# A running logsumexp along time: three steps per partition, Exp written over its input, and one stream of chunks

## The chip, the core and the metric

One core of one Trainium2 chip. The time is device microseconds of one launch; medians of several runs are given. The profile's span is about 1.8 us shorter than the time of the run.

The engines' names: PE is the matrix engine, ACT the one that computes Exp and Ln, DVE the vector engine, SP the one whose queue issues all DMA transfers here. "The DMA records of the trace" are the starts, durations and sizes of the single packets that the 16 DMA engines moved. What I say of single packets is read from these. They don't name the engine.

## The reference

```python
# x: (4, 4096, 4128) float32, standard normal
out[:, 0, :] = x[:, 0, :]
for t in range(1, S):
    mx = np.maximum(out[:, t - 1, :], x[:, t, :])
    out[:, t, :] = mx + np.log(np.exp(out[:, t - 1, :] - mx) + np.exp(x[:, t, :] - mx))
```

That is a running sum of exp(x) along time, and its logarithm. 270.5 MB are read and 270.5 MB written.

## The kernel before

A tile holds R = 2 consecutive time steps on each of 128 partitions, so a partition's part of a transfer is one run of 2 x 4128 x 4 = 33,024 B. ACT writes Exp in fp16 to its own buffers; PE adds along the partitions with triangular matrices of ones (`incl`, `excl`), adds the running sum of the tiles before (`pick` times `carry`) and, for the second step, the second row (`ident`); ACT takes Ln from PSUM into the tile; DVE saves the last row's sum in two fp16 parts (`keep`).

```python
R = 2
xpool = ctx.enter_context(tc.tile_pool(name="xpool", bufs=5))
epool = ctx.enter_context(tc.tile_pool(name="epool", bufs=4))
# ... (cut)
class Step:
    def __init__(self, b, k):
        self.xt = xpool.tile([P, R, D], FP32, name="xt")
        self.dram = lambda t: t[b, k * rows:(k + 1) * rows, :].rearrange("(p j) d -> p j d", j=R)
        nc.sync.dma_start(out=self.xt, in_=self.dram(x))          # load
    def exp(self, c):
        et = epool.tile([P, R, CH + tail], FP16, name="et")
        nc.scalar.activation(et[:, :, :w], self.xt[:, :, s], ACT.Exp)
    # ... (cut: head, second, tail)
    def ln(self, j, c):
        nc.scalar.activation(self.xt[:, j, c * CH:(c + 1) * CH], self.pt[c], ACT.Ln)
    def store(self):
        nc.sync.dma_start(out=self.dram(out), in_=self.xt)
    def run(self):                       # one tile from its first Exp to its store
        self.exp(0); self.head(0)
        for c in range(1, n_main):
            ...                          # (cut)
        self.store()

for i, (b, k) in enumerate(work):        # 64 tiles
    if i == 0:
        steps += [Step(*work[n]) for n in range(3)]
    if i + 3 < len(work):
        steps.append(Step(*work[i + 3])) # the load of tile i+3 stands before the store of tile i
    steps[i].run()
```

The softmax here doesn't subtract the row's maximum and nothing guards it: scores larger than these inputs give would overflow.

## Time and profile before

| | before |
|---|---|
| time, median | 1265.67 us (three runs, 1265.14 to 1265.82) |
| bytes moved by DMA | 541 MB |
| ACT, PE, DVE busy | 962.5, 663.4, 655.7 us of 1263.8 |
| data packets | 16,384 of 33,024 B, median 1222 ns |

From the profile's page of the kernel before: span, busy times, moved GB/s in 40 slices, the data queue (packets with the completions, MB, share of the engines' time), the chain that ended last, the Exp instructions (count, busy us, mean ns; then idle time before them and its cause), and the transfers with their median time from issue to landing.

```profile
span 1263.8 us, 7025 instructions
...
PE 663.4 (52%) x2392; PEld 242.3 (19%) x2392; DVE 655.7 (52%) x645; ACT 962.5 (76%) x833; POOL 2.2 (0%) x13
...
GB/s 401 418 433 429 434 431 430 433 431 432 430 435 434 430 434 432 434 431 431 432 434 434 432 433 433 432 431 434 434 429 434 435 433 429 433 435 431 431 435 322
...
q1 hardware_dynamic: 18432, 541.07, 99.4%
...
DMA 81%; ACT 2%; issue 1%; PE 1%; DVE 1%; SPq 1%; ACTq 0%
...
L111 ACT ACTIVATE et<-xt 128x2048 f16<-128x2048 f32 (+1 forms) x256 | 485.4, 1921 | 152.8 <-DMA xt<-in_x_dram 152.8
...
xt<-in_x_dram SPq DMA_DIRECT2D x64, 4128.0 KB, 29.4
out_dram<-xt SPq DMA_DIRECT2D x64, 4128.0 KB, 38.8
```

Nearly every slice moves 429 to 435 GB/s; only the first two (401 and 418) and the last (322) fall behind. No compute engine is busy for more than 76% of the span, and ACT's largest idle time before Exp is a wait for loads. The chain is 81% DMA. Each load lands 29.4 us after its issue though a transfer of this size takes 4128 x 1024 B / 432 GB/s = 9.8 us: about two others lie before it in the queue.

A stretch of 200 us in the middle (its length; busy us and count of each engine; granted PE clock; DMA busy share; GB/s):

```profile
core 0: us, PE busy (x) PEld busy (x) DVE busy (x) ACT busy (x) POOL busy (x), PEclk, DMA share, GB/s
900.00:1100.00 200.00, 104.72 (x379) 38.41 (x380) 104.33 (x103) 152.72 (x133) 0.00 (x0) 0.77 1.00 432
```

DMA is busy all of the time at 432 GB/s. The same view of the end of the run:

```profile
1230.00:1240.00 10.00, 5.62 (x24) 2.03 (x23) 4.91 (x4) 7.90 (x8) 0.00 (x0) 0.83 0.99 429
1240.00:1245.00 5.00, 0.51 (x2) 0.02 (x1) 4.05 (x5) 1.82 (x3) 0.00 (x0) 0.72 1.01 438
1245.00:1250.00 5.00, 0.00 (x0) 0.00 (x0) 1.25 (x2) 0.00 (x0) 0.00 (x0) 0.50 0.98 423
1250.00:1255.00 5.00, 0.00 (x0) 0.00 (x0) 0.00 (x0) 0.00 (x0) 0.00 (x0) 0.50 0.87 376
1255.00:1260.00 5.00, 0.00 (x0) 0.00 (x0) 0.00 (x0) 0.00 (x0) 0.00 (x0) 0.50 0.28 119
```

The rate falls step by step after 1250 us: the 16 DMA engines do not finish together. In the DMA records they finish between 1250.9 and 1260.7 us after the first packet, the slowest 9.8 us behind the first.

### The profile page before, as it was taken

To read this page: it belongs to the slowest core of one execution; us is meant where nothing else is said; L and a number is where in the kernel's file an instruction comes from. 1 tells how busy PE (TensorE), PEld (TensorE's weight loads), DVE (VectorE), ACT (ScalarE), POOL (GpSimd) and SP (SyncE) were. 2 spreads that over 40 slices of the span, in tenths; PEclk is the share of its full clock that TensorE was granted. 3 is DMA by queue.
4 is the path that set the end of the run, shared out by engine and by line. 5 is a ranking of instruction groups with operands and counts; after the bars stand their busy time and mean duration, and the time that the engine had idled before them with its cause. 6 is when DMAs were issued, how large, how long until landed. Compare 5 with 4: busy or idle time off the path is not lost.

```text
span 1263.8 us, 7025 instructions
## 1 busy us (share of the span) xinstructions
PE 663.4 (52%) x2392; PEld 242.3 (19%) x2392; DVE 655.7 (52%) x645; ACT 962.5 (76%) x833; POOL 2.2 (0%) x13
## 2 busy tenths in 40 slices
PE   3665655545545465464454655556445464554541
PEld 1222222211112121121121211112112121121210
DVE  3566565464454544645546455464564544545443
ACT  5889887778678787786877877778778787787872
POOL 0000000000000000000000000000000000000000
PEclk8878788778687777777867777777777777777876
DMA  9999999999999999999999999999999999999997
GB/s 401 418 433 429 434 431 430 433 431 432 430 435 434 430 434 432 434 431 431 432 434 434 432 433 433 432 431 434 434 429 434 435 433 429 433 435 431 431 435 322
DMA packets 18466, 541.51 MB, mean 428 GB/s; under 512 B 2048, under 2 KB 2048, under 8 KB 2048
## 3 DMA queue, kind: packets, MB, share of 16 engines
q1 hardware_dynamic: 18432, 541.07, 99.4%
q8 instruction: 19, 0.31, 0.1%
q14 instruction: 15, 0.12, 0.0%
HBM read 270.53 MB, written 270.53 MB: 428 GB/s over the span
## 4 chain that ended last, share of the span: by engine, by line
DMA 81%; ACT 2%; issue 1%; PE 1%; DVE 1%; SPq 1%; ACTq 0%
DMA out_dram<-xt 74%; DMA xt<-in_x_dram 7%; ACT xt L126 1%; ACT et L111 1%; PE pt L86 1%; SPq L102 1%; DVE carry L90 0%; DVE carry L91 0%; SPq L153 0%; DVE carry_t L90 0%; DVE carry_t L91 0%; ACTq L126 0%
## 5 line engine op out<-in xcount | busy, mean ns | idle before, releaser
L90 DVE CAST carry<-pt 32x1024 f16<-32x1024 f32 x256 | 314.9, 1230 | 576.4 <-ACT xt L126 573.3
L111 ACT ACTIVATE et<-xt 128x2048 f16<-128x2048 f32 (+1 forms) x256 | 485.4, 1921 | 152.8 <-DMA xt<-in_x_dram 152.8
L126 ACT ACTIVATE xt<-pt 128x1024 f32<-128x1024 f32 x512 | 504.2, 1028 | 125.8 <-PE pt L86 64.9
L86 PE MATMUL pt<-et,incl 128*128 128x512 f16 x512 | 211.6, 506 | 549.4 <-ACT et L111 386.0
L91 DVE TENSOR_TENSOR carry<-pt,carry 32x1024 f16<-32x1024 f32 x256 | 314.0, 1226 | 8.9
L86 PE MATMUL pt<-et,excl 128*128 128x512 f16 x512 | 211.3, 505 | 0.0
L86 PEld LDWEIGHTS <-incl 128*128 128x128 f16 x704 | 69.0, 111 | 684.7 <-issue 631.9
L86 PE MATMUL pt<-carry,pick 128*128 128x512 f16 x480 | 195.2, 498 | 0.0
L86 PE MATMUL pt<-et,ident 128*128 128x512 f16 x512 | 174.4, 426 | 27.7 <-ACT xt L126 27.7
L86 PEld LDWEIGHTS <-excl 128*128 128x128 f16 x576 | 71.2, 124 | 116.1 <-issue 83.9
L86 PEld LDWEIGHTS <-pick 128*128 128x128 f16 x600 | 69.5, 118 | 94.4 <-issue 66.0
L86 PEld LDWEIGHTS <-ident 128*128 128x128 f16 x512 | 49.5, 106 | 102.4 <-issue 76.4
L86 PE MATMUL qt<-et,incl 128*128 128x32 f16 x192 | 19.6, 189 | 0.0
L86 PE MATMUL qt<-carry_t,pick 128*128 128x32 f16 x120 | 15.6, 182 | 0.0
L149 ACT ACTIVATE xt<-qt 128x64 f32<-128x64 f32 x64 | 14.6, 228 | 0.0
L90 DVE CAST carry_t<-qt 32x32 f16<-32x32 f32 x64 | 12.6, 197 | 2.0
L91 DVE TENSOR_TENSOR carry_t<-qt,carry_t 32x32 f16<-32x32 f32 x64 | 12.4, 193 | 2.2
L86 PE MATMUL qt<-et,excl 128*128 128x32 f16 x64 | 11.6, 182 | 0.0
L81 DVE MEMSET carry<- 128x512 uint32 x4 | 1.9, 485 | 1.1 <-PEq L199 1.0
L68 ACT ACT_TABLE_LOAD x1 | 1.3, 1283 | 0.8 <-PEq L199 0.8
L35 POOL TENSOR_SCALAR_AFFINE_SELECT pick<-pick 128x128 f16<-128x128 f16 x2 | 0.6, 292 | 0.1
L25 POOL TENSOR_SCALAR_AFFINE_SELECT incl<-incl 128x128 f16<-128x128 f16 x1 | 0.3, 293 | 0.0
(11 smaller groups left out, 1.9 us busy)
## 6 DMA issues: line engine op xcount, KB each, us to landing
xt<-in_x_dram SPq DMA_DIRECT2D x64, 4128.0 KB, 29.4
out_dram<-xt SPq DMA_DIRECT2D x64, 4128.0 KB, 38.8
```

The lines of the kernel that those rows point to most:

```text
L25: nc.gpsimd.affine_select(out=t, in_=t, pattern=[[1, P]], compare_op=mybir.AluOpType.is_ge, fill=0.0, base=base, channel_multiplier=-1,)
L35: nc.gpsimd.affine_select(out=t, in_=t, pattern=[[step, P]], compare_op=mybir.AluOpType.not_equal, fill=1.0, base=base, channel_multiplier=1,)
L68: nc.scalar.preload_act_table_set("natural_log_exp_and_others")
L81: nc.vector.memset(t, 0.0)
L86: nc.tensor.matmul(pt, lhsT=w, rhs=rhs, start=start, stop=stop, skip_group_check=True)
L90: nc.vector.tensor_copy(cr[HI:HI + 32, :], pt[HI:HI + 32])
L91: nc.vector.tensor_tensor(out=cr[LO:LO + 32, :], in0=pt[HI:HI + 32], in1=cr[HI:HI + 32, :], op=mybir.AluOpType.subtract,)
L102: nc.sync.dma_start(out=self.xt, in_=self.dram(x))
L111: nc.scalar.activation(et[:, :, :w], self.xt[:, :, s], ACT.Exp)
L126: nc.scalar.activation(self.xt[:, j, c * CH:(c + 1) * CH], self.pt[c], ACT.Ln)
L149: nc.scalar.activation(self.xt[:, :, t0:D], self.qt, ACT.Ln)
```

## The change

The intent was longer runs, so fewer packets and transfers. Three time steps per partition make runs of 49,536 B. To fit four such tiles in SBUF, Exp writes its fp16 result over the first half of the chunk's own float32 bytes, and the Exp buffers go. The chunks of all tiles form one stream, in which Exp runs two chunks ahead, across tile borders. 32 groups of 128 rows are not divisible by three: each batch has ten tiles of three rows and one of two, 44 tiles instead of 64. The diff, cut to its core:

```diff
-R = 2
+R = 3
-    xpool = ctx.enter_context(tc.tile_pool(name="xpool", bufs=5))
-    epool = ctx.enter_context(tc.tile_pool(name="epool", bufs=4))
+    bufs = 4
+    xpool = ctx.enter_context(tc.tile_pool(name="xpool", bufs=bufs))
@@ Exp over its input
-            et = epool.tile([P, R, CH + tail], FP16, name="et")
-            nc.scalar.activation(et[:, :, :w], self.xt[:, :, s], ACT.Exp)
+            nc.scalar.activation(
+                self.t.half[:, :, 2 * c0:2 * c0 + w], self.t.xt[:, :, c0:c0 + w], ACT.Exp,
+            )
@@ one stream of chunks   (cut: head, stage, the tile list)
-        steps[i].run()
+    ahead = bufs - 1
+    for s in steps[:ahead]:
+        s.load()
+    chunks[0].exp()
+    chunks[1].exp()
+    chunks[0].head()
+    for g in range(len(chunks) + R - 1):
+        for d in range(R - 1, -1, -1):
+            if 0 <= g - d < len(chunks) and d < chunks[g - d].t.r:
+                k = chunks[g - d]
+                k.stage(d)
+                if k.c == last and d + 1 == k.t.r:
+                    k.t.store()
+                    if stored + ahead < len(steps):
+                        steps[stored + ahead].load()
+                    stored += 1
+        if g + 2 < len(chunks):
+            chunks[g + 2].exp()
+        if g + 1 < len(chunks):
+            chunks[g + 1].head()
```

The load of tile i+3 now stands behind the store of tile i.

## The prediction

> What bounds the kernel now: the 16 DMA engines. The page's slices show DMA at 9 in all but the last slice and 430 to 435 GB/s almost throughout, except the first (401) and last (322). The table of stretches gives a DMA share of 1.00 and 432 or 433 GB/s in each 200 us stretch from 100 to 1100 us. The chain that ended last is 81% DMA. The compute engines have slack: ACT 76% (962.5 us), PE 52%, DVE 52%; ACT idles 152.8 us waiting for loads (groups list). In the trace's DMA records each of the 16,384 data packets (one 33,024 B run) has a median of 1222 ns: 27.02 B/ns, or 432.4 GB/s on 16 engines. So each engine works 1024 x 1.222 = 1251.3 us on data, plus 128 completion packets of 9 ns (1.2 us). The other 11 us of the 1263.8 us span are the start, collisions with instruction fetches, and a ragged end in which the engines finish at different times (376, 119, then 17 GB/s after 1250 us).
>
> What the change does:
> - Bytes: unchanged, 541 MB. No gain there.
> - Packets: 704 per engine instead of 1024, of 49,536 B (33,024 B in the short tiles). The Trainium skill, "DMA: Bandwidth & Descriptors", "Where 436 GB/s comes from", gives 16 ports x 32 B x 850 MHz. From it I estimate 1214 ns for 33,024 B, so the measured 1222 ns leaves about 8 ns fixed per packet. Then a 49,536 B packet takes about 1829 ns: 640 x 1.829 + 64 x 1.222 = 1249 us, a saving of 2.3 us; 40 fewer completions save 0.4 us.
> - Alignment: 49,536 is 193.5 x 256, so every second run starts 128 B off a 256 B boundary (before, none did). The same page, "How a descriptor splits into AXI transactions", makes that 4 extra beats; I estimate 5 ns on half of the packets, 1.5 us given back.
> - ACT: Exp is one instruction of 3 x 1024 instead of 2 x 1024 (1901 ns now; estimate 2.8 us), 512 Ln of 1028 ns stay. DVE keeps the carry 44 times instead of 64 per chunk: 655 us falls to about 450. PE: about the same total. All this is off the critical path: worth nothing.
> - Buffers: four of 49.5 KB, three loads ahead. A load waits for the previous tile's store, and a store waits for Exp of the next tile's first two chunks. By my count the queue still holds about two transfers (14.6 us each) whenever the next is issued, and a store is ready some 10 us after the next tile's load, with 29 us to spare. At the start three loads cover 41 us and the first store comes at about 36. No new bubble.
>
> On the critical path lies only the per-packet cost: net 1 to 3 us of 1265.
>
> Predicted: 1263.5 us, 8 in 10 between 1257 and 1270. Faster by over 2%: 0.02; within 2%: 0.95; slower by over 2%: 0.03.
>
> What would show it: q1 data packets 11,264 instead of 16,384; packet median near 1830 ns; stretches still 432 to 434 GB/s at share 1.00; DVE near 450 us; ACT still waiting for loads; load landing about 44 us, store about 58 us instead of 29.4 and 38.8.
>
> What would make it wrong: larger packets running at another rate (unaligned HBM writes dearer than a few beats, or another fixed cost per packet); a bubble in the DMA queue, slices below 425 GB/s, because the load waits in order behind a store that waits for the next tile's Exp; engines finishing more unevenly.

## More of the kernel before

I followed each engine through packets that begin where another ends, so numbers of one engine are a reconstruction. "Mean idle time" is the time without a packet under way, averaged over the 16 engines; it needs no such following.

Last, what SP's queue waited for (us in total, times, longest):

```profile
SPq L102 <- DMA out_dram<-xt: 1079.6, 59, 19.2
SPq L153 <- ACT xt L126: 90.5, 8, 18.2
```

SP waits for a buffer, that is, for an earlier store to land, and only rarely for ACT. Stores are ready well before the queue gets to them.

## The result, and the profile after

The changed kernel took 1262.84 us (median of 4 runs, 1262.66 to 1263.26) against 1265.69 us for the kernel before in the same rounds. The ratio is 0.9979, 95% interval 0.9961 to 0.9996: 2.8 us less, the same within 2%. A repetition on another occasion gave 1263.02 against 1265.59 us, again 0.9979.

The same parts of the page, for the changed kernel:

```profile
span 1261.0 us, 6165 instructions
...
PE 688.7 (55%) x2268; PEld 237.0 (19%) x2268; DVE 451.4 (36%) x445; ACT 947.3 (75%) x733; POOL 2.2 (0%) x13
...
GB/s 411 410 439 431 432 427 434 438 430 432 433 437 431 432 432 436 432 427 436 431 433 436 437 429 431 436 436 432 430 434 435 432 431 432 434 435 431 433 422 347
DMA packets 12702, 541.46 MB, mean 429 GB/s; under 512 B 1408, under 2 KB 1408, under 8 KB 1408
...
q1 hardware_dynamic: 12672, 541.07, 99.4%
...
DMA 69%; ACT 21%; PE 5%; issue 2%; DVE 1%; SPq 0%; ACTq 0%
...
L128 ACT ACTIVATE xt<-xt 128x3072 f16<-128x3072 f32 (+3 forms) x176 | 478.5, 2719 | 247.9 <-DMA xt<-in_x_dram 247.8
...
xt<-in_x_dram SPq DMA_DIRECT2D x40, 6192.0 KB, 42.2
out_dram<-xt SPq DMA_DIRECT2D x40, 6192.0 KB, 28.1
```

The slices still show 427 to 439 GB/s nearly throughout; the first two and the last two are lower. Of the 12,672 packets of the data queue 1408 are completions, 16 for each of the 88 transfers, and 11,264 carry data. DVE fell from 655.7 to 451.4 us and ACT from 962.5 to 947.3 us, and neither mattered. A load lands 42.2 us after its issue, three transfers of 14.6 us. A store lands 28.1 us after its issue, two transfers of that size, where the kernel before had four smaller ones.

The middle (columns as before):

```profile
900.00:1100.00 200.00, 109.86 (x361) 38.01 (x361) 72.18 (x72) 151.67 (x118) 0.00 (x0) 0.77 1.00 433
```

The same busy share and the same rate. The end:

```profile
1230.00:1240.00 10.00, 6.73 (x22) 2.31 (x22) 7.75 (x8) 9.29 (x9) 0.00 (x0) 0.83 0.63 269
1240.00:1245.00 5.00, 1.90 (x12) 0.72 (x10) 4.84 (x6) 3.13 (x4) 0.00 (x0) 0.93 1.08 466
1245.00:1250.00 5.00, 0.00 (x0) 0.00 (x0) 1.64 (x2) 0.00 (x0) 0.00 (x0) 0.50 0.98 423
1250.00:1255.00 5.00, 0.00 (x0) 0.00 (x0) 0.00 (x0) 0.00 (x0) 0.00 (x0) 0.50 0.98 423
1255.00:1260.00 5.00, 0.00 (x0) 0.00 (x0) 0.00 (x0) 0.00 (x0) 0.00 (x0) 0.50 0.73 317
```

Here is something that was not there before. The rate falls to 269 GB/s between 1230 and 1240 us, recovers, and then stops at once, without the long thinning out. What SP waited for:

```profile
SPq L116 <- ACT xt L162: 1178.4, 44, 30.0
SPq L113 <- DMA out_dram<-xt: 14.3, 4, 4.9
```

SP waits for ACT, almost all of the time, and hardly ever for a buffer: the stores have become late. The chain near the end of the run (start us, duration, what) says why:

```profile
1124.26 42.48 DMA xt<-in_x_dram
...
1166.77 2.76 ACT xt L128
...
1183.04 37.65 DMA xt<-in_x_dram
```

A load is issued at 1124.26 us and lands at 1166.75. ACT's time line after it (start us, us, instruction; in brackets the idle time before it; L128 is Exp, L162 is Ln):

```profile
1166.77 2.76 ACT L128 ACTIVATE xt<-xt 128x3072 f16<-128x3072 f32 x1 [6.10 <-DMA xt<-in_x_dram]
...
1173.52 2.75 ACT L128 ACTIVATE xt<-xt 128x3072 f16<-128x3072 f32 x1
...
1178.88 2.79 ACT L128 ACTIVATE xt<-xt 128x3072 f16<-128x3072 f32 x1
1181.54 2.87 ACT L162 ACTIVATE xt<-pt 128x1024 f32<-128x1024 f32 x3
```

Three Exp of the new tile run, with Ln of the older one between them. Only after the first of the last three Ln shown comes the store of the older tile, at 1182.61 us, with the next load behind it, as SP's own time line says:

```profile
37.00 0.35 SPq L116 DMA_DIRECT2D out_dram<-xt  x1
...
1153.25 0.34 SPq L116 DMA_DIRECT2D out_dram<-xt  x1
1153.68 0.38 SPq L113 DMA_DIRECT2D xt<-in_x_dram  x1
1182.61 0.34 SPq L116 DMA_DIRECT2D out_dram<-xt  x1
1183.04 0.38 SPq L113 DMA_DIRECT2D xt<-in_x_dram  x1
```

A store is issued 1182.61 - 1166.75 = 15.9 us after the next tile's load has landed. The order of the code agrees: before the last Ln of a tile stand three Exp of the next one, not two.

From the DMA records, the median duration of a packet by its size, in all kernels:

```
bytes    ns     seen in
 8,256   312    one-engine experiment (runs start on 256 B boundaries)
16,512   615    the two padded kernels
33,024  1222    before, and the short tiles after
49,536  1829    after
```

From 33,024 to 49,536 B it is 607 ns more, 27.20 B/ns, which on 16 engines is 435.2 GB/s. That is just the ceiling in the Trainium skill, "DMA: Bandwidth & Descriptors", "Where 436 GB/s comes from". On this line 33,024 B alone take 1214 ns, so about 8 ns of each packet don't depend on its size.

### The profile page after: what moved, and what is told of

Its sections match the earlier page's. It is cut to its first block, busy times and chain, and to the rows that moved or that the text cites. A ratio compares the mean times of both kernels' runs of the same rounds, so it can differ in the third digit from the quotient of the medians.

```text
span 1261.0 us, 6165 instructions
## 1 busy us (share of the span) xinstructions
PE 688.7 (55%) x2268; PEld 237.0 (19%) x2268; DVE 451.4 (36%) x445; ACT 947.3 (75%) x733; POOL 2.2 (0%) x13
## 2 busy tenths in 40 slices
DMA packets 12702, 541.46 MB, mean 429 GB/s; under 512 B 1408, under 2 KB 1408, under 8 KB 1408
## 3 DMA queue, kind: packets, MB, share of 16 engines
q1 hardware_dynamic: 12672, 541.07, 99.4%
## 4 chain that ended last, share of the span: by engine, by line
DMA 69%; ACT 21%; PE 5%; issue 2%; DVE 1%; SPq 0%; ACTq 0%
DMA xt<-in_x_dram 67%; ACT xt L128 11%; ACT xt L162 10%; PE pt L88 5%; DMA out_dram<-xt 2%; ACT xt L167 0%; SPq L116 0%; DVE carry L92 0%; DVE carry L93 0%; ACTq L231 0%; SPq L113 0%; ACTq L128 0%; PE qt L88 0%
## 5 line engine op out<-in xcount | busy, mean ns | idle before, releaser
L128 ACT ACTIVATE xt<-xt 128x3072 f16<-128x3072 f32 (+3 forms) x176 | 478.5, 2719 | 247.9 <-DMA xt<-in_x_dram 247.8
L88 PE MATMUL pt<-xt,ident 128*128 128x512 f16 x672 | 251.3, 470 | 530.7 <-ACT xt L162 530.4
L162 ACT ACTIVATE xt<-pt 128x1024 f32<-128x1024 f32 x512 | 487.6, 1030 | 2.5 <-PE pt L88 0.7
L92 DVE CAST carry<-pt 32x1024 f16<-32x1024 f32 x176 | 216.4, 1230 | 761.0 <-ACT xt L162 760.7
L88 PE MATMUL pt<-xt,excl 128*128 128x512 f16 x672 | 247.0, 504 | 0.0
L93 DVE TENSOR_TENSOR carry<-pt,carry 32x1024 f16<-32x1024 f32 x176 | 215.9, 1227 | 6.1
L88 PE MATMUL pt<-xt,incl 128*128 128x512 f16 x352 | 152.0, 526 | 23.6 <-ACT xt L128 15.0
L88 PEld LDWEIGHTS <-excl 128*128 128x128 f16 x756 | 92.5, 124 | 141.0 <-issue 108.1
L88 PE MATMUL pt<-carry,pick 128*128 128x512 f16 x320 | 109.8, 429 | 0.0
L88 PEld LDWEIGHTS <-incl 128*128 128x128 f16 x480 | 45.2, 111 | 129.7 <-DVE carry L93 95.2
L88 PEld LDWEIGHTS <-pick 128*128 128x128 f16 x360 | 40.6, 113 | 57.0 <-issue 34.3
## 6 DMA issues: line engine op xcount, KB each, us to landing
xt<-in_x_dram SPq DMA_DIRECT2D x40, 6192.0 KB, 42.2
out_dram<-xt SPq DMA_DIRECT2D x40, 6192.0 KB, 28.1
```

What stands on the lines that cost most here:

```text
L88: nc.tensor.matmul(pt, lhsT=w, rhs=rhs, start=start, stop=stop, skip_group_check=True)
L92: nc.vector.tensor_copy(cr[HI:HI + 32, :], pt[HI:HI + 32])
L93: nc.vector.tensor_tensor(out=cr[LO:LO + 32, :], in0=pt[HI:HI + 32], in1=cr[HI:HI + 32, :], op=mybir.AluOpType.subtract,)
L128: nc.scalar.activation(self.t.half[:, :, 2 * c0:2 * c0 + w], self.t.xt[:, :, c0:c0 + w], ACT.Exp,)
L162: nc.scalar.activation(t.xt[:, j, c * CH:(c + 1) * CH], pt, ACT.Ln)
```

## The experiments

Theory: the DMA engines' own work (packets and transfers) gained the time, and the slowest DMA engine sets the end. Rivals: the new order of compute or the in-place Exp gained it; or mean DMA idle time near the end counts, so that the new hole costs something. Times below are medians, with the kernel before in the same rounds at 1265.4 to 1265.6 us.

### Copies without compute, two and three rows

```diff
-    chunks = [Chunk(s, c) for s in steps for c in range(n_main)]
-    # ... the stream
+    for i, s in enumerate(steps):
+        s.store()
+        if i + ahead < len(steps):
+            steps[i + ahead].load()
```

Their outputs are wrong, which doesn't matter for the times. The first has R = 2, the second R = 3, both four buffers.

> Only the loads and stores of the changed kernel with two rows per partition (33,024 B packets); no compute, so the result is wrong on purpose. Packet theory (the change saved about 8 ns on each of 320 packets and 9 ns on each of 40 completions per engine): packets 1222 ns, 1024 per engine, and the time is 2.9 us (2.5 to 3.3) above the copy with three rows. Rival (the saving came from the new order of work or its instructions, not from the packets): the two copies agree within 1 us. Absolute time about 1259 us if instruction fetches are what makes engines finish unevenly, 1263 or more if they are not.

> The same copy with three rows per partition (49,536 B packets). Packet theory: 1829 ns a packet, about 1256 us, 2.9 us below the copy with two rows. Rival: same time as the copy with two rows within 1 us.

Measured: 1262.44 us (1261.31 to 1263.47) with two rows, 1258.31 us (1257.69 to 1258.74) with three, 4.1 us apart. The rival's "within 1 us" fails: the gain exists with no compute at all. But 4.1 us is more than the 2.5 to 3.3 us expected of packets and completions. The two profiled copies are 5.9 us apart: packets are under way 1.7 us less on the mean engine, and the other 4.2 us are mean idle time (6.5 us against 2.3), nearly all of it at the end, where engines that are done wait for the slowest. And 1262 rather than 1259 us with two rows says that instruction fetches aren't what makes the engines uneven: this copy has almost none (14 small fetch packets, 3 us in all; the kernel before has 49, 26 us), and its engines still finished 8 us apart. So the prediction's list for the remaining 11 us was not complete.

### The stream with two rows

```diff
-R = 3
+R = 2
-    bufs = 4
+    bufs = 5
-    ahead = bufs - 1
+    ahead = 3
```

> The changed kernel with two rows per partition instead of three (five buffers, three loads ahead as before): Exp over x and one stream of chunks stay, packets are again 33,024 B. Packet theory: as the kernel before, 1265.7 us, within 1 us. Rival (the stream or Exp in place gained it): near the changed kernel, 1262.8 us.

Measured: 1272.14 us (1270.41 to 1272.54), ratio 1.0050 to the kernel before. Neither expectation held: it is 6.6 us slower than before. The page's slices and transfers:

```profile
GB/s 400 383 432 433 431 432 427 432 433 433 431 433 433 432 433 433 433 428 432 433 433 433 433 432 433 432 432 433 433 433 433 433 431 434 432 433 433 433 428 300
...
xt<-in_x_dram SPq DMA_DIRECT2D x64, 4128.0 KB, 31.0
out_dram<-xt SPq DMA_DIRECT2D x64, 4128.0 KB, 21.6
```

The middle runs at 432 GB/s as ever, but the second slice has 383 and the last 300. A store lands 21.6 us after its issue, against 38.8 in the kernel before with the same transfers: nearly two transfers fewer lie before it in the queue. In the DMA records all 16 engines are idle at once for 4.0 us of this run, and for no time in the kernel before and the changed one. Mean idle time is 10.2 us, 2.2 of it in the first 100 us, against 6.3 us in the kernel before: 3.9 of the 4.9 us by which the two profiled runs differ. So the stream and the in-place Exp gained nothing by themselves. They make stores later. That the longer transfer is what makes up for it is my reading; no run tests it by itself.

### The last tile not streamed into

```diff
+    stream(chunks[:-n_main])     # the loop as it was, on all tiles but the last
+    stream(chunks[-n_main:])
```

> The changed kernel, but the last short tile is not streamed into: the tile before it is finished and stored first, without waiting for the last load. In the changed kernel's trace the store before last came late and 15 of 16 DMA engines stood idle some microseconds near the end (4 us of mean idle). If the mean idle time counts: up to 4 us faster, about 1259 us. If the slowest DMA engine alone sets the end (it was never idle): same as the changed kernel, 1262.8 us, within 0.7 us; the hole in the GB/s at 1230 to 1240 us goes, and a ragged end comes in its place.

Measured: 1262.70 us (1262.69 to 1263.11), ratio 0.9977, against 0.9979 for the changed kernel. That is the number of the slowest-engine reading, but this run can't decide between the two. The windows show the hole moved rather than gone, so the expectation was only half right here, and mean idle time over the last 60 us is the same, 4.7 us against 4.8 in the changed kernel:

```profile
1230.00:1240.00 10.00, 6.92 (x16) 2.26 (x16) 3.94 (x4) 8.27 (x7) 0.00 (x0) 0.50 1.01 438
1240.00:1245.00 5.00, 3.89 (x12) 1.35 (x11) 2.47 (x3) 3.54 (x4) 0.00 (x0) 0.67 0.81 347
1245.00:1250.00 5.00, 1.64 (x11) 0.58 (x9) 3.96 (x5) 2.87 (x4) 0.00 (x0) 1.00 0.38 165
```

The rate holds from 1230 to 1240 us now and falls from 1240 to 1250 us instead, where the last store is not ready. The DMA records of the changed kernel show why the hole is free: 15 engines ran out of work between 1227.6 and 1233.8 us and restarted together at 1234.5 us. The sixteenth was still at work on the store before, ended it at 1235.12 us and went straight on into the next one. It did not wait in the hole, and at the end it was still 0.7 us behind the others. Whether the slowest engine or the mean sets the time is tested further down, by extra work on one engine.

### The same bytes in smaller packets

```diff
 # padded changed kernel; the padded kernel before likewise
-            full = xpool.tile([P, R, D], FP32, name="xt")
-            self.xt = full[:, :self.r, :]
+            full = xpool.tile([P, R, D + 16], FP32, name="xt")
+            self.xt = full[:, :self.r, :D]
 # column halves, in place of the single transfer, for loads and stores
+            h = D // 2
+            nc.sync.dma_start(out=self.xt[:, :, :h], in_=self.dram(x)[:, :, :h])
+            nc.sync.dma_start(out=self.xt[:, :, h:], in_=self.dram(x)[:, :, h:])
```

> The changed kernel with 64 B of padding behind each row in SBUF, so that a partition's three rows are three runs of 16,512 B; bytes, order and completions stay. Packet theory (7 to 8 ns fixed per packet): packets of about 615 ns, 2048 instead of 704 per engine, 1248.8 becomes 1259.5 us of packets per engine: 10.7 us slower than the changed kernel, about 1273.5 us. Rival (packet size does not matter): 1262.8 us.

> The kernel before with the same padding: two runs of 16,512 B per partition. Packet theory: 2048 packets per engine as in the padded changed kernel, 8.2 us slower than before, about 1273.9 us, and within 1 us of the padded changed kernel, as only 40 completions of 9 ns are left between them. Rival (order or in-place Exp gained): the padded before stays 2.5 us or more above the padded changed one.

> The changed kernel with every transfer split into two column halves: runs of 8,256 B, 4096 packets per engine, 176 completions. Packet theory: about 311.5 ns a packet, 27 to 28 us slower than the changed kernel, about 1290.7 us. Rival with no fixed cost: 1263 us; a cost that grows faster than the packet count would give more than 1295 us.

| kernel | packet | packets per engine | time us | more per added packet |
|---|---|---|---|---|
| changed (rounds of the result) | 49,536 B | 704 | 1262.84 | |
| changed, padded | 16,512 B | 2048 | 1272.58 | 9.7 us / 1344 = 7.2 ns |
| changed, column halves | 8,256 B | 4096 | 1293.69 | 30.9 us / 3392 = 9.1 ns |
| before, same rounds | 33,024 B | 1024 | 1265.40 | |
| before, padded | 16,512 B | 2048 | 1274.45 | 9.1 us / 1024 = 8.8 ns |

The slices of the padded changed kernel, then those of the kernel with column halves:

```profile
GB/s 392 421 430 429 428 429 431 430 427 430 430 430 429 430 430 430 429 430 430 430 428 429 431 430 430 428 430 430 429 428 429 432 423 431 429 431 430 430 420 346
```

```profile
GB/s 389 419 424 423 423 423 423 424 423 423 423 423 423 424 422 423 424 423 423 422 425 422 424 423 424 422 423 423 422 423 423 424 423 424 424 424 422 423 393 332
```

The level of the whole run falls with the packet size, to 430 and to 423 GB/s. So a fixed cost per packet is real, and with 7 to 9 ns of run time it is near what the packet durations give. Two expectations were missed. The column halves came out 3 us above theirs; their median packet is 314 ns, where 311.5 was expected. And the padded pair, which moves the same packets, still differs by 1.9 us, where 0.4 us was expected and 1 us allowed. Something besides packet size favours the changed kernel. In the profiled pair it is idle time: packets are under way for 1262.1 us on the mean engine in the changed kernel and 1261.8 us in the one before, and mean idle time is 5.4 us against 7.3. Whether this comes from fewer transfers or from the new order of compute, the pair can't tell, as it differs in both.

### Extra work on one DMA engine

```diff
             nc.sync.dma_start(out=self.xt, in_=self.dram(x))
+            more = dpool.tile([1, D // 2], FP32, name="more")
+            nc.sync.dma_start(out=more, in_=x[b, k * rows:k * rows + 1, :D // 2])
```

This is on the kernel before.

> The kernel before plus, with every tile, one extra load of 8,256 B into a single partition, which should run on a single DMA engine: 64 x (312 + 9) ns = 20.5 us more work on that engine, 0.1% more bytes in all. If the slowest engine sets the time: 11 to 20 us slower (less than the whole by what that engine had to spare, at most about 9 us), 1277 to 1286 us. If the mean over the engines sets it: 1.3 us slower, 1267 us.

Measured: 1287.09 us (1285.76 to 1288.87), 21.7 us slower for 20.5 us of added packets and 0.1% more bytes. The records have 64 packets of 8,256 B and 64 more completions, so each extra load used one DMA engine. The Trainium skill, "DMA: Bandwidth & Descriptors", "Why a DMA increments its semaphore by 16 and not by 1", says that software can split a contiguous one-row transfer into an outer dimension so that it spreads over engines. Here it is not split, and each went as one packet. The end of the run:

```profile
1250.00:1260.00 10.00, 6.87 (x30) 2.71 (x29) 3.64 (x3) 8.33 (x7) 0.00 (x0) 0.84 0.70 301
1260.00:1270.00 10.00, 1.73 (x7) 0.25 (x3) 6.58 (x8) 2.97 (x4) 0.00 (x0) 0.67 0.64 275
1270.00:1280.00 10.00, 0.00 (x0) 0.00 (x0) 0.00 (x0) 0.00 (x0) 0.00 (x0) 0.50 0.41 178
```

The busy share sinks to 0.41 while the loaded engine works on alone; the other engines ended together, 10.7 us before it. The time goes with the slowest engine. The mean over the engines, which would have cost 1.3 us, does not set it. The run is 1.1 us above the expected range, which had allowed for an engine with time to spare: what that engine had to spare was nothing that could be seen.

### Fewer change-overs between reading and writing

In the copies' records, the time above the median packet sits at the borders of transfers. With two rows the eight packets of a transfer on an engine have mean durations of 1226.9, 1222.0, 1222.1, 1222.0, 1222.2, 1222.2, 1226.0 and 1239.1 ns. It falls mostly on a few engines: the slowest collected about 9 us in the copy with two rows and 5.4 us in that with three, where most engines have 2 to 3 us. I took the change from load to store for the cause.

```diff
-    for i, s in enumerate(steps):
-        s.store()
-        if i + ahead < len(steps):
-            steps[i + ahead].load()
+    for i in range(0, len(steps), 2):
+        steps[i].store()
+        steps[i + 1].store()
+        for s in steps[i + bufs:i + bufs + 2]:
+            s.load()
```

> The copy with two rows per partition, but two loads, then two stores, and so on: same packets, same number of transfers, half as many change-overs between reading and writing (result wrong on purpose). In the traces so far the time over the median packet sits mostly in the first and last packet of a transfer, and on a few engines far more than on the others (up to 9 us over the run in the copy). If the change-over between load and store causes it: the slowest engine gains 2 to 4 us, 1258.5 to 1260.5 us against 1262.4. If each transfer causes it, whatever its neighbour: 1262.4 us, within 1 us.

> The same pairing in the copy with three rows per partition. Change-over theory: the slowest engine had 5.4 us over the median packet, about half of it goes, 1255.5 to 1257 us against 1258.3. Transfer theory: 1258.3 us within 1 us.

> The changed kernel with stores and loads in pairs (store, store, load, load; four loads at the start); bytes, packets and compute stay. The queue stays full by my count, the hole before the last store goes too. Change-over theory: the slowest engine loses 1 to 2.5 us of its excess, 1260.3 to 1261.8 us. Transfer theory: 1262.8 us within 0.7 us. A new hole in the queue would show as slices under 425 GB/s and more than 1263.5 us.

> The changed kernel itself once more, on the same chip as the paired variants: 1262.8 us within 0.5 us by every theory.

Measured: the paired copies took 1261.82 us (unpaired 1262.44) and 1257.93 us (unpaired 1258.31). Half of the change-overs gone is worth 0.4 to 0.6 us, not 2 to 4, and even that is less than the spread of the unpaired copies' own runs (2.2 and 1.1 us). That theory fell, for the most part. Whether it is the border of any transfer, or the number of transfers, these runs don't tell.

The changed kernel in pairs took 1267.04 us (1266.41 to 1267.37), 4 us slower than the changed kernel beside it (1263.02 us). Its windows near the end show ACT as busy as it can be and the queue short of work:

```profile
1200.00:1220.00 20.00, 10.67 (x34) 3.63 (x34) 7.76 (x8) 18.44 (x14) 0.00 (x0) 0.72 1.01 436
1220.00:1240.00 20.00, 11.02 (x47) 3.88 (x46) 11.22 (x11) 19.29 (x18) 0.00 (x0) 0.97 0.77 333
```

The expectation's count, that the queue stays full, was wrong. Loads that land in pairs bring ACT's work in pairs: ACT was busy for 19.29 of the 20 us in which DMA sank to 333 GB/s. No variant beat the changed kernel.

## Why the prediction was right or wrong

The time was right: 1263.5 us was predicted, 1262.84 measured, inside 1257 to 1270, and "within 2%" had 0.95. Point by point:

- **"What bounds the kernel now: the 16 DMA engines."** Right: the copy without compute is only 3 us faster than the kernel before with two rows, and 4.5 us faster than the changed one with three. It has to be sharpened: the slowest of the 16 sets the time (20.5 us more work on one cost 21.7 us).
- **"about 8 ns fixed per packet".** Right: four packet sizes lie on one line, and smaller packets cost 7 to 9 ns of run time each. Packets of 1829 ns were predicted and measured. But consecutive packets of an engine overlap by 3 to 4 ns in the records, and the prediction simply added durations. With 8 - 3.2 = 4.8 ns, 320 fewer packets are worth 1.5 us rather than 2.3 us (an estimate from the records); by the run time per added packet they would be worth 2.3 to 2.9 us.
- **Alignment, "1.5 us given back".** Wrong: this term is not there. Half of the 49,536 B runs start off a 256 B boundary, but 8,299 of the 10,240 packets took exactly 1829 ns, and the median is 1829 at each of the eight places in a transfer, odd or even. It was taken from the Trainium skill, "How a descriptor splits into AXI transactions", which the trace doesn't bear out at this size.
- **"On the critical path lies only the per-packet cost: net 1 to 3 us."** Half right, and the number holds partly by luck. The prediction's own terms (2.3, 0.4 and -1.5 us) come to 1.2 us, and 2.8 were measured. The two profiled runs, also 2.8 us apart, divide it: packets are under way for 1254.4 us on the mean engine before and 1252.9 us after, 1.5 us less; mean idle time is 6.3 us before and 5.0 us after, 1.3 us less. (A second profile of the changed kernel has 1253.2 and 5.0 us.) So about half of the gain is packets, and about half comes from engines that finish more evenly, which the prediction had only as a risk in the other direction. Why the slowest engine is less late stays open.
- **ACT, DVE and PE "worth nothing".** Right: DVE lost 204 us of work, and copies without compute show the gain too. DVE about 450 us and loads landing at about 44 us were near (451.4, 42.2).
- **Buffers: "the queue still holds about two transfers" and a store "some 10 us after the next tile's load".** Wrong, this is the step that failed. A store comes 15.9 us after that load, for three Exp of the next tile stand before it and not two, and one transfer is then in the queue. Stores land after 28.1 us; "about 58 us" had been predicted. The copy with three rows, whose stores wait for no compute, does have 58.1 us.
- **"No new bubble."** Wrong at the end: 269 GB/s from 1230 to 1240 us. It cost nothing, because the slowest engine was not idle in it and still ended last. With two rows the stream is 6.6 us slower than the kernel before, most of it as idle time at the start and at the end. The start was counted right: first store about 36 us, measured 37.0.

## What to carry to other kernels

When DMA is at its rate throughout, look for what is left in its own records: a fixed cost per packet can be read from two packet sizes, and it says what longer runs can give (here some 1.5 of 1265 us). Judge a hole in the transfer rate by the slowest DMA engine, not by the mean, since a hole that only the faster engines see is free. When a stream runs ahead across tile borders, count what stands before each store in program order, because lateness that costs nothing with long transfers can cost time with shorter ones (the stream with two rows, 6.6 us).

## What the Trainium skill lacked or had wrong

- "DMA: Bandwidth & Descriptors", "Where 436 GB/s comes from": confirmed, within the 1 ns resolution of the records, by the slope between two packet sizes (607 ns for 16,512 B on 16 engines, 435.2 GB/s). The page has no measured fixed cost of a long packet on this queue: about 8 ns of each duration, of which 3 to 4 ns overlap with the next packet, and 7 to 9 ns of run time per added packet. "Why small descriptors are slow" on the same page gives about 3 cycles per packet, which at 850 MHz is 3.5 ns (an estimate from the page).
- The same page, "How a descriptor splits into AXI transactions": extra beats for a run that starts off a 256 B boundary don't show with runs of 49,536 B (median 1829 ns at every place in a transfer). With 8,256 B runs, of which three in four start off the boundary, the median is 314 ns and 312 is the most frequent duration, as in runs that start on the boundary; no run here tells reads from writes in that.
- No page has a figure for how far the 16 engines of one queue drift apart under equal work. They finished up to 9.8 us apart in the kernel before and 8 us apart in a copy that had almost no instruction fetches; the extra time sits in the first and last packets of transfers. Pairing loads and stores hardly changed the time (0.4 to 0.6 us), so the cause is open.
